# A two-layer hybrid trunk on one core: conditioning loads on GpSimd's queue, output products behind the inner products of their turn, half a unit between the token transposes

## The chip, the cores and the metric

The kernel runs on one core of a Trainium2 chip. A core has five engines with one instruction stream each: TensorE (PE; its weight loads are listed as PEld), VectorE (DVE), ScalarE (ACT), GpSimd (POOL) and SyncE (SP). Each works through its own stream in order, and waits on semaphores where an instruction needs the result of another engine. Transfers are issued from an engine's stream and run on 16 DMA engines that are shared by all streams.

The metric is the device time of one execution in microseconds (us). A difference is judged from several runs of both kernels on the same chip.

## The reference

One sequence of 256 tokens of width 1024 goes through two layers. Each layer has three sub-layers: a feed-forward block (SwiGLU), a token mixer, and a second feed-forward block. The mixer of layer 0 is HGRN2, a gated linear recurrence with eight heads; that of layer 1 is a chunked gMLP. All sub-layers have the same frame, where shift, scale and gate come from a vector c of the sequence:

```
cond = silu(c)
mod = (cond @ ada_w[i] + ada_b[i]).reshape(B, 3 * N_SUB, D_MODEL)[:, :, None, :]
...
def swiglu(h, w_in, w_out):
    a, b = jnp.split(h @ w_in, 2, axis=-1)
    return (jax.nn.silu(a) * b) @ w_out

def sublayer(x, fn, pre_g, post_g, shift, scale, gate, res_w):
    h = rms_norm(x, pre_g) * (1.0 + scale) + shift
    return x + res_w * gate * rms_norm(fn(h), post_g)
```

The computation of `mod` is called the conditioning here. Its weights are 1024 x 9216 numbers for each layer, and each is used once. All data are float32.

## The kernel before

**Sub-layers.** The six sub-layers are called ffn0, hg, ffn1, ffn2, gm and ffn3, and are worked off one after the other. The 256 tokens are two tiles of 128 (t = 0, 1). Between two sub-layers stands the seam: `tail` scales the output y and adds it to x for each token tile, and `prenorm` normalizes x, transposes it on PE (`npa`), applies scale and shift on ACT (`hf`, L243) and splits it into two parts (`h`, L247 and L248).

**Products in split form.** Float32 operands are split into a rounded part (hi) and the rest (lo), and a product is hi*hi + hi*lo + lo*hi. A weight block of 1 MB comes as two loads of 512 KB into `raw` (4 buffers); ACT casts each into the hi part (L119), and DVE subtracts to get lo (L120). `next_block` (`nb`) hands out the blocks in the order in which the host laid them out. Split blocks lie in the pool `whl` of 12 tiles, two tiles a block.

**Conditioning.** It is 144 products: a tile of 128 outputs x 1024 weights (512 KB, `ada`) is loaded, and DVE multiplies it with `cond` and sums along the row (L169), which gives one column of `mod`. `pace(upto, blocks, skip)` sets a rate, and `wblock` calls `ada` at that rate, so that the products are written between the weight blocks. All loads of weights and of conditioning are issued by SP through `load` (L55), and `keep_in_program_order` holds each behind whatever was traced before it on the same engine. The conditioning tiles lie in the pool `adap` of two buffers; the first 16 products also use the four buffers of `p4` for two tiles out of three (`ring`). The HGRN2 gate's scratch tile `L` (L526) takes its buffers from `adap` too.

**A feed-forward layer.** The inner width of 2816 is cut into 11 units of 256. In ffn0 the units 0 to 3 are made in eight steps over the inner dimension, as the conditioning of the first norm arrives. In ffn1, ffn2 and ffn3 the units 0 and 1 are made by `proj` with the tokens as rows, since token tile 0 is ready before tile 1; it fills the four PSUM banks of the pool `acc`. `post_tok` then takes silu and product, token tile by token tile, and transposes the result on PE (`tps`, L396) into the form that the output product needs; ACT and DVE split it (L147, L148). The other units go through `unit2`, a generator with two steps: each makes two chunks of 128 columns (`chunk2`, the `ups` matmuls of L328 and L329), whose banks are read by ACT and DVE (L377 to L382). After the inner products of a turn, `out()` adds an older unit's output products (`y`, L142 to L144) into four y banks, until no more than two units are pending:

```
for u in range(len(pend), 11):
    ...
    while len(pend) > 2:
        out()
```

In turn u == 8 `gate_tile` makes the gate of the sub-layer as a row: a transpose on PE (`gps`), a copy (`grow`), a transfer to memory (`gflat`, L199) and one that spreads the row over all partitions (`G`, L201). Both transfers are issued by POOL, which does nothing else after the start.

**What sets the order.** The semaphores and the order of each engine's instructions come from a planner that simulates the program: of the instructions whose operands are ready by its reckoning it takes the one written first, so an instruction may run far ahead of, or behind, its place in the program. `after` adds an edge of issue order alone. `paced` uses it: the first matmul of a group is placed behind the instruction in `self.gate`, if one is set, and the gate is cleared.

Of the kernel before, what the change touches and what calls it, by code (L numbers as in the profile page):

```python
# [10 lines left out]
F32 = mybir.dt.float32  # L11
# [7 lines left out]
P = 128  # L19
D = 1024  # L20
S = 256
KC = D // P
# [11 lines left out]
class Body:  # L34
    def __init__(self, ctx, tc, ins, out):
        self.ctx, self.tc, self.nc, self.out = ctx, tc, tc.nc, out
        self.d = dict(zip(_INS, ins))
        pool = lambda name, bufs, **k: ctx.enter_context(tc.tile_pool(name=name, bufs=bufs, **k))
        self.const = pool("const", 1)
        self.raw = pool("raw", 4)  # L40
        self.whl = pool("whl", 12)
        self.act = pool("act", 1)
        self.adap = pool("adap", 2)
        self.cols = pool("cols", 2)
        self.tiny = pool("tiny", 4)
        self.bcp = pool("bcp", 2)
        self.p4 = pool("p4", 4)
        self.p2 = pool("p2", 4)
        self.scr = pool("scr", 1)
        self.acc = pool("acc", 4, space=PSUM)  # L50
        self.yps = pool("yps", 1, space=PSUM)
        self.dram = pool("dram", 2, space=bass.MemoryType.DRAM)
# [106 lines left out]
    def ada(self, upto):  # L159
        nc = self.nc  # L160
        while self.ada_next < min(upto, 144):
            i = self.ada_next
            if self.ring and i % 3:
                t = self.p4.tile([P, D], F32, tag="t4", name="ada")
            else:
                t = self.adap.tile([P, D], F32, tag="ada", name="ada")
            self.load(t, self.d["ada"][i])
            junk = self.scr.tile([P, D], BF16, tag="junkv", name="junkv")
            nc.vector.tensor_tensor_reduce(junk, t, self.cond, 1.0, 0.0, ALU.mult, ALU.add,  # L169
                                           self.mod[i // 24][:, i % 24:i % 24 + 1])  # L170
            self.ada_next += 1
# [150 lines left out]
    def chunk2(self, w, c):  # L322

        ps = self.acc.tile([P, 2, S], F32, tag="acc", name="ups")
        mm = self.nc.tensor.matmul
        for kc in range(KC):
            u = [x[:, kc * 256 + c * P:kc * 256 + (c + 1) * P] for x in w]
            self.paced(mm(ps, u[0], self.h2[:, :, :, kc, :], start=kc == 0, stop=False))  # L328
            mm(ps[:, 1, :], u[1], self.h2[:, 0, :, kc, :], start=False, stop=kc == KC - 1)  # L329
        return ps  # L330

    def mm3f(self, o, u, h, start, stop):
        mm = self.nc.tensor.matmul
        self.paced(mm(o, u[0], h[0], start=start, stop=False))  # L334
        mm(o, u[0], h[1], start=False, stop=False)  # L335
        mm(o, u[1], h[0], start=False, stop=stop)  # L336

    def gtile(self):

# [1 line left out]
        return [g[:, i * 512:(i + 1) * 512].rearrange("p (k s) -> p k s", k=2) for i in range(2)]  # L341

    def out_unit(self, y, gT, wo, first):
        for t in range(NT):
            for h in range(2):
                for k in range(2):
                    self.out_mm(y[t][h], t, h, gT, k, wo, k, first and k == 0, False)

# [9 lines left out]
    def ffn(self, f, hT, G_fn, pre_next, nxt, bg):  # L358
        nc = self.nc
        state = {"out": 0}  # L360
        nb = self.next_block
# [25 lines left out]

        def post_tok(pa, pb):
            gTs = [self.gtile() for _ in range(2)]
            for t in range(NT):  # L390
                sa = self.t2()
                self.tact(sa, pa[t], AF.Silu)
                nc.vector.tensor_mul(sa, sa, pb[t])
                ps = self.acc.tile([P, 512], F32, tag="acc", name="tps")
                for k in range(4):
                    nc.tensor.transpose(ps[:, k * P:(k + 1) * P], sa[:, k * P:(k + 1) * P], self.ident)  # L396
                pv = ps.rearrange("p (u k s) -> p u k s", u=2, k=2)
                for u in range(2):
                    self.split_ps(*[g[:, :, t * P:(t + 1) * P] for g in gTs[u]], pv[:, u])
            return gTs  # L400

        def out():
            self.out_unit(y, pend.pop(0), nb(), state["out"] == 0)
# [20 lines left out]
            self.late_consts()  # L424
        else:
            wa, wb = [[nb(), nb()] for _ in range(2)]
            pend = post_tok(*self.proj(hT, [wa, wb], 512, split=True))
        y = self.y_banks()
        self.pace(bg, 25 if f == 0 else 26)
        for u in range(len(pend), 11):  # L430
            if f == 0:
                pa = self.unit(hT, nb())
                pb = self.unit(hT, nb())
            else:
                steps = unit2(nb(), nb())
                next(steps)
                next(steps)
            while len(pend) > 2:
                out()
            if f == 0:  # L440
                pend.append(post(pa, pb))
            else:
                for _ in steps:
                    pass
            if u == 8:
                G = G_fn()
# [38 lines left out]
    def hgrn(self, hT, G_fn, pre_next, nxt, bg):  # L485
# [37 lines left out]

        def gate_f(hb, pr, z):

            L = self.adap.tile([P, 512], F32, tag="ada", name="L")  # L526
            c = slice(512 * pr, 512 * pr + 512)
            k, nk, b = kn[hb][:, c], kn[hb][:, H4:][:, c], bq[hb][:, c]
            nc.scalar.activation(L, z, AF.Abs)
# [246 lines left out]
    def gmlp(self, hT, G_fn, pre_next, nxt, bg):  # L776
# [12 lines left out]
            self.tact(o, o, AF.Gelu_apprx_tanh)  # L789

        v, vt = [], []
        self.pace(bg, 30, 6)
        for j in range(6):
            if j == 0:
                bbs = [bcast(self.t2(N), "gbin", N * i) for i in range(2)]
# [300 lines left out]
```

## Time and profile before

| | |
|---|---|
| time, median of 3 runs | 1191.67 us (1189.63 to 1193.36) |
| the profiled execution | 1193.24 us, span 1191.5 us |
| granted TensorE clock, mean | 0.984 |
| moved by DMA | 282.32 MB, mean 237 GB/s |
| conditioning loads | 144 of 512 KB, issued by SP |
| weight loads | 376 of 512 KB, issued by SP |

The span is the time from the first to the last instruction; the profiled execution's own time is 1.7 us longer. The profile gives the busy time of each engine, the transfers, the chain of work that ended last, and for each idle stretch of an engine who ended it. In such a row "PE y L142 <- ACT t L147: 4.5, 3, 2.4" says that PE, at the instruction of line 142 that writes y, waited for ACT's instruction of line 147 that writes t: 4.5 us in total, three times, 2.4 us at most. A timeline row has the start and the length in us, the engine, the line, the operation, what it writes and reads, and in brackets the idle time before it with who ended it. SPq and PEq are the sequencers of SP and PE.

### The profile page before, as it was taken

The page shows a single profiled execution, that of the slowest core. Times are in us where ns is not written, and L with a number is a line of the kernel's source. Part 1 is how long each engine was busy: PE and PEld are TensorE (multiplying, and loading weights), DVE is VectorE, ACT ScalarE, POOL GpSimd, SP SyncE. Part 2 cuts the span into 40 slices and gives each one's busy share as a digit, 9 for nine tenths or more (in the row PEclk, how much of TensorE's full clock was granted, in tenths as well). Part 3 has the DMA queues.
Part 4 walks back from the last instruction along what each step waited for, and adds up shares of the span by engine and source line. Part 5 has one row for each costly group of instructions (what it writes and reads, how often), then busy time and mean ns, then how long its engine had stood idle before and what let it go on. Part 6 is the DMA issues. An engine that isn't in the chain of part 4 may idle for free.

```text
span 1191.5 us, 17180 instructions
## 1 busy us (share of the span) xinstructions
PE 1146.5 (96%) x6518; PEld 995.4 (84%) x6518; DVE 888.8 (75%) x1331; ACT 657.2 (55%) x1054; POOL 6.8 (1%) x16
## 2 busy tenths in 40 slices
PE   7999999997997999999999999999999999999997
PEld 6999998797895788888778888888888887888886
DVE  6997888868887887787677787657978786666652
ACT  6464446648766754456655545554754457555541
POOL 0000000000000000000000000000000000000000
PEclk9999999997999999999999999999999999999999
DMA  9899998782335777887578888537777765666640
GB/s 345 311 314 318 333 327 314 251 285 101 124 95 185 263 267 272 278 272 262 173 251 267 282 269 272 188 124 261 277 254 262 248 212 177 203 222 233 213 137 36
DMA packets 79765, 282.32 MB, mean 237 GB/s; under 512 B 9873, under 2 KB 10561, under 8 KB 79682
## 3 DMA queue, kind: packets, MB, share of 16 engines
q1 hardware_dynamic: 78626, 278.05, 68.0%
q0 software_dynamic: 1056, 3.17, 0.8%
q8 instruction: 51, 0.84, 0.3%
q14 instruction: 32, 0.26, 0.1%
HBM read 280.11 MB, written 1.07 MB: 236 GB/s over the span
## 4 chain that ended last, share of the span: by engine, by line
PE 73%; DMA 10%; DVE 8%; ACT 5%; issue 3%; SPq 0%; DVEq 0%; ACTq 0%
PE ups L328 15%; PE ups L329 8%; PE y L144 7%; PE y L142 7%; PE y L143 7%; PE ups L418 4%; DMA ada<-in_ada 4%; DMA raw<-in_wffn 4%; DVE w L120 3%; PE ups L334 3%; PE ups L336 3%; PE ups L335 3%; DMA raw<-in_whg 3%; ACT w L119 2%; PE ab L599 2%
## 5 line engine op out<-in xcount | busy, mean ns | idle before, releaser
L120 DVE TENSOR_TENSOR w<-raw,w 128x1024 fp32r<-128x1024 f32 x376 | 453.5, 1220 | 84.7 <-ACT w L119 77.5
L119 ACT CAST w<-raw 128x1024 fp32r<-128x1024 f32 x376 | 388.0, 1050 | 202.9 <-DMA raw<-in_wffn 79.4
L328 PE MATMUL ups<-h,w 128*128 128x512 f32 x864 | 303.1, 394 | 0.0
L169 DVE CUSTOM_DVE_ANT_0 junkv<-ada,cond 128x1024 bf16<-128x1024 f32 x144 | 175.8, 1221 | 92.0 <-DMA ada<-in_ada 91.5
L329 PE MATMUL ups<-h,w 128*128 128x256 f32 x864 | 242.5, 281 | 0.0
L328 PEld LDWEIGHTS ups<-h,w 128*128 128x128 f32 x864 | 162.3, 188 | 36.8
L142 PE MATMUL y<-w,t 128*128 128x512 f32 x448 | 179.4, 400 | 4.5 <-ACT t L147 4.5
L143 PE MATMUL y<-w,t 128*128 128x512 f32 x448 | 178.2, 398 | 0.0
L144 PE MATMUL y<-w,t 128*128 128x512 f32 x448 | 177.6, 397 | 0.2
L329 PEld LDWEIGHTS ups<-h,w 128*128 128x128 f32 x864 | 163.7, 190 | 0.9
L334 PE MATMUL ups<-h,w 128*128 128x256 f32 x416 | 118.3, 285 | 0.6 <-ACT w L119 0.6
L336 PE MATMUL ups<-h,w 128*128 128x256 f32 x416 | 117.8, 283 | 0.2 <-DVE w L120 0.2
L335 PE MATMUL ups<-h,w 128*128 128x256 f32 x416 | 117.6, 283 | 0.0
L142 PEld LDWEIGHTS y<-w,t 128*128 128x128 f32 x448 | 84.5, 189 | 24.1 <-ACT t L147 5.3
L144 PEld LDWEIGHTS y<-w,t 128*128 128x128 f32 x448 | 84.3, 189 | 21.0 <-DVE t L148 1.1
L143 PEld LDWEIGHTS y<-w,t 128*128 128x128 f32 x448 | 84.5, 189 | 17.9
L79 ACT ACTIVATE t<-t 128x256 f32<-128x256 f32 (+2 forms) x70 | 36.3, 523 | 97.7 <-DVE t L378 95.5
L334 PEld LDWEIGHTS ups<-h,w 128*128 128x128 f32 x416 | 79.7, 192 | 1.7 <-ACT w L119 0.8
L335 PEld LDWEIGHTS ups<-h,w 128*128 128x128 f32 x416 | 79.7, 192 | 0.8 <-issue 0.2
L336 PEld LDWEIGHTS ups<-h,w 128*128 128x128 f32 x416 | 79.7, 192 | 0.4 <-DVE w L120 0.4
L291 PE MATMUL pps<-w,h 128*128 128x512 f32 x160 | 64.4, 403 | 5.3 <-DVE h L247 5.3
L292 PE MATMUL pps<-w,h 128*128 128x512 f32 x160 | 63.8, 399 | 0.0
(199 smaller groups left out, 1435.4 us busy)
## 6 DMA issues: line engine op xcount, KB each, us to landing
raw<-in_wffn SPq DMA_DIRECT2D x264, 512.0 KB, 5.5
ada<-in_ada SPq DMA_DIRECT2D x144, 512.0 KB, 6.5
raw<-in_wgmu SPq DMA_DIRECT2D x48, 512.0 KB, 5.2
raw<-in_whg SPq DMA_DIRECT2D x40, 512.0 KB, 5.8
raw<-in_wgmv SPq DMA_DIRECT2D x24, 512.0 KB, 5.0
G<-gflat POOLq DMA_DIRECT2D x6, 512.0 KB, 5.9
t<-in_gbin SPq DMA_DIRECT2D x6, 256.0 KB, 5.2
x<-in_x SPq DMA_DIRECT2D x2, 512.0 KB, 4.0
```

Of the source, the lines that this page charges most:

```text
L119: nc.scalar.copy(hi[:, sl], raw)
L120: nc.vector.tensor_sub(lo[:, sl], raw, hi[:, sl])
L142: self.paced(mm(ps, l[0], r[0], start=start, stop=False))
L143: mm(ps, l[0], r[1], start=False, stop=False)
L144: mm(ps, l[1], r[0], start=False, stop=stop)
L169: nc.vector.tensor_tensor_reduce(junk, t, self.cond, 1.0, 0.0, ALU.mult, ALU.add, self.mod[i // 24][:, i % 24:i % 24 + 1])
L291: mm(res[g][t], h(0, kc), u(0, kc), start=kc == 0, stop=False)
L328: self.paced(mm(ps, u[0], self.h2[:, :, :, kc, :], start=kc == 0, stop=False))
L329: mm(ps[:, 1, :], u[1], self.h2[:, 0, :, kc, :], start=False, stop=kc == KC - 1)
L334: self.paced(mm(o, u[0], h[0], start=start, stop=False))
L335: mm(o, u[0], h[1], start=False, stop=False)
L336: mm(o, u[1], h[0], start=False, stop=stop)
```

## The change

It has five edits.

- The conditioning loads are issued by POOL instead of SP, held in order among what POOL issues. The pool `adap` has three buffers instead of two.
- `L` of the HGRN2 gate has its own buffer in a new pool `lp` for the second pair of heads, and the scratch tile `hf` for the first.
- `chunk2` and `mm3f` note their last matmul in `self.last`. `out_unit` sets it as the gate before each group of output products, so that they are issued behind the inner products written last.
- In ffn1, ffn2 and ffn3 `post_tok` is a generator. The first step of unit 2 is written between the first and the second token tile; the turn of u == 2 then has only the second step left.
- The rates: ffn0 spreads its products over 22 weight blocks (before 25), the other feed-forward layers over 23 (before 26), with the rate set ahead of unit 2's blocks, and the gMLP layer over 27 (before 30).

```diff
-        self.adap = pool("adap", 2)
+        self.adap = pool("adap", 3)
+        self.lp = pool("lp", 1)
...
-            self.load(t, self.d["ada"][i])
+            self.tc.keep_in_program_order(nc.gpsimd.dma_start(t, self.d["ada"][i]))
...
-            mm(ps[:, 1, :], u[1], self.h2[:, 0, :, kc, :], start=False, stop=kc == KC - 1)
+            self.last = mm(ps[:, 1, :], u[1], self.h2[:, 0, :, kc, :], start=False, stop=kc == KC - 1)
...
-        mm(o, u[1], h[0], start=False, stop=stop)
+        self.last = mm(o, u[1], h[0], start=False, stop=stop)
...
     def out_unit(self, y, gT, wo, first):
         for t in range(NT):
             for h in range(2):
+                self.gate = self.last
                 for k in range(2):
                     self.out_mm(y[t][h], t, h, gT, k, wo, k, first and k == 0, False)
...
         def post_tok(pa, pb):
             gTs = [self.gtile() for _ in range(2)]
+            pend.extend(gTs)
             for t in range(NT):
...
-            return gTs
+                yield
...
             wa, wb = [[nb(), nb()] for _ in range(2)]
-            pend = post_tok(*self.proj(hT, [wa, wb], 512, split=True))
+            pend = []
+            self.pace(bg, 23)
+            tokens = post_tok(*self.proj(hT, [wa, wb], 512, split=True))
+            next(tokens)
+            steps = unit2(nb(), nb())
+            next(steps)
+            next(tokens)
         y = self.y_banks()
-        self.pace(bg, 25 if f == 0 else 26)
+        if f == 0:
+            self.pace(bg, 22)
         for u in range(len(pend), 11):
...
-                steps = unit2(nb(), nb())
-                next(steps)
+                if u > 2:
+                    steps = unit2(nb(), nb())
+                    next(steps)
                 next(steps)
...
-            L = self.adap.tile([P, 512], F32, tag="ada", name="L")
+            L = self.lp.tile([P, 512], F32, tag="L", name="L") if pr else self.scr.tile([P, 512], F32, tag="hf", name="L")
...
-        self.pace(bg, 30, 6)
+        self.pace(bg, 27, 6)
```

## The prediction

> **What bounds the kernel now.** I read the page first, then the busy time in stretches, the waits of each engine, and only then the chain of waits around the places that the first three point to.
>
> ```profile
> span 1191.5 us, 17180 instructions
> PE 1146.5 (96%) x6518; PEld 995.4 (84%) x6518; DVE 888.8 (75%) x1331; ACT 657.2 (55%) x1054; POOL 6.8 (1%) x16
> ```
>
> TensorE (PE) is idle for 1191.5 - 1146.5 = 45.0 us; no matmul is added or taken away, so nothing here can be worth more than that. The stretches tell where the idle time lies. The columns are the stretch, its length, then busy time and count of PE, its weight loads, VectorE (DVE), ScalarE (ACT) and GpSimd (POOL), then clock, DMA share and GB/s.
>
> ```profile
> 190.00:300.00 110.00, 99.88 (x628) 91.22 (x626) 87.25 (x144) 71.77 (x129) 0.00 (x0) 0.94 0.65 217
> 300.00:390.00 90.00, 82.03 (x487) 70.69 (x486) 75.20 (x129) 62.05 (x127) 1.07 (x2) 0.96 0.41 135
> ...
> 420.00:555.00 135.00, 135.00 (x722) 115.82 (x721) 102.38 (x149) 67.53 (x108) 1.08 (x2) 1.00 0.79 271
> 555.00:620.00 65.00, 59.54 (x261) 47.58 (x260) 46.57 (x73) 38.90 (x71) 0.00 (x0) 0.95 0.65 220
> ```
>
> The body of a feed-forward layer (420 to 555) leaves PE no gap at all: faster weights or products are worth nothing there. The time is lost at seams, where one sub-layer hands over to the next (555 to 620), and in the HGRN2 layer. Who ended PE's waits (us in total, times, longest):
>
> ```profile
> PE pps L291 <- DVE h L247: 5.3, 5, 2.3
> PE y L142 <- ACT t L147: 4.5, 3, 2.4
> ...
> PE npa L239 <- DVE xn L233: 3.2, 2, 2.1
> PE fps L336 <- DVE w L120: 3.1, 2, 1.7
> PE ab L599 <- DVE t L593: 3.0, 1, 3.0
> ...
> PE npa L239 <- ACT xn L235: 1.7, 2, 1.2
> PE vps L854 <- DVE t L861: 1.6, 2, 1.2
> PE tps L396 <- DVE t L393: 0.9, 1, 0.9
> PE fps L334 <- ACT w L119: 0.7, 1, 0.7
> ```
>
> These rows are the prices of what follows.
>
> **Part 1: the first turn of ffn1, ffn2 and ffn3 (output products gated, a unit's step between the transposes).** The three waits of y for the cast L147 are the three starts of these layers. The order in time for ffn2, on PE and on ACT:
>
> ```profile
> 606.30 0.60 PE L396 MATMUL tps<-ident,t 128*128 128x128 f32 x4
> 609.32 0.50 PE L142 MATMUL y<-w,t 128*128 128x512 f32 x1 [2.43 <-ACT t L147]
> ...
> 612.39 0.78 PE L328 MATMUL ups<-h,w 128*128 128x512 f32 x1
> ```
> ```profile
> 607.96 1.04 ACT L119 CAST w<-raw 128x1024 fp32r<-128x1024 f32 x1 [2.11 <-DMA raw<-in_wffn]
> 608.91 0.36 ACT L147 CAST t<-tps 128x256 fp32r<-128x256 f32 x1
> ```
>
> After token tile 0's transposes PE's next instruction is an output product, which needs L147; L147 stands on ACT behind a weight cast that waits 2.11 us for its DMA. The inner products (ups), whose operands are ready, are queued behind it until 612.39. The change forbids that order and traces half a unit between the transposes. That half is 32 matmuls (two chunks, eight k, two each), at 135 / 722 = 187 ns about 6.0 us: more than the 2.43 us that they have to cover, and than the 0.9 us for token tile 1's multiplication L393. So both rows go: 4.5 + 0.9 = **-5.4 us**. It adds no instruction and no semaphore, only issue order. What it needs is a PSUM bank: of the four "acc" banks the projection holds all, and two come free when token tile 0's silu and multiplication have read them, before its transposes; I see no reason for a new stall. Bounds: 0 (no bank, or the unit's weights late) to -5.4. In later turns, and in ffn0 and the gMLP layer, the gate orders only what the program order already has; where PE has no idle time there is nothing to lose, and I take 0. If a unit's weights came late there, the output products queued behind its last inner product would no longer fill in; that cover is the full PE of the 420 row.
>
> **Part 2: the conditioning loads leave SP.** The 144 products of the conditioning (L169) and their loads remain; each load is issued by POOL instead of SP. Waits of SP's queue, and of DVE for these loads:
>
> ```profile
> SPq L56 <- DVE w L120: 588.0, 246, 19.1
> ...
> SPq L56 <- DVE mod L169: 77.2, 42, 6.2
> ```
> ```profile
> DVE junkv L169 <- DMA ada<-in_ada: 91.5, 51, 5.4
> ```
>
> For 77.2 us SP stood at a conditioning load whose buffer a product had not freed, with weight loads behind it. Here is what that does at the seams, from the chain of waits (start, length, what):
>
> ```profile
> 198.03 1.23 DVE junkv L169
> ...
> 199.72 6.83 DMA raw<-in_whg
> ```
> ```profile
> 257.38 0.94 DVE junkv L169
> ...
> 258.97 5.01 DMA raw<-in_whg
> ```
> ```profile
> 565.03 6.61 DMA ada<-in_ada
> ...
> 571.66 1.23 DVE junkv L169
> ```
> ```profile
> 868.77 6.58 DMA ada<-in_ada
> ```
>
> At 565 the load went out behind weight loads; DVE stands until 571.66 in the middle of a tail, and PE pays the 2.1 us of the longest npa wait. With loads on their own queue, a third buffer, and the pace ended about three weight blocks sooner (23 for 26), the load is long there: **-2.1** (bounds 0 to -2.1). At 199.72 and 258.97 a weight load leaves only after a product has freed a buffer. The first ends in PE's longest wait for h (2.3) and in the one for ACT's xn (1.2); the weight buffers might hold these loads as well, so I take half of 3.5: **-1.7** (0 to -3.5). The second feeds the waits of fps (3.1 + 0.7); in that stretch ACT also loses 3.9 us because L, the gate's scratch, shares the two conditioning buffers, and the change gives L buffers of its own:
>
> ```profile
> ACT L L529 <- DVE mod L169: 3.9, 1, 3.9
> ```
>
> With either cause gone the weights come sooner by more than the 3.8 us: **-3.8** (0 to -6.8, if the 3.0 of L599 just after goes too). The wait at 868 is the vps row: **-1.6** (0 to -1.6). Moving L to the scratch tile "hf" makes it wait for the last prenorm, done by then: nothing; without that it would be the same 3.9.
>
> The pace (22 for 25, 23 for 26, 27 for 30 blocks) moves products and changes no count. The issue costs POOL, idle 99%, about what its own loads of the same 512 KB cost:
>
> ```profile
> 156.12 0.65 POOL L199 DMA_DIRECT2D gflat<-grow  x1 [155.67 <-ACT grow L197]
> 162.88 0.56 POOL L201 DMA_DIRECT2D G<-gflat  x1 [6.11 <-DMA gflat<-grow]
> ```
> ```profile
> ada<-in_ada SPq DMA_DIRECT2D x144, 512.0 KB, 6.5
> G<-gflat POOLq DMA_DIRECT2D x6, 512.0 KB, 5.9
> ```
>
> 144 x 0.56 = 81 us on an idle engine, and a landing no later than SP's: 0. By the Trainium skill's "DMA: Bandwidth & Descriptors", section "Issuing engines are not separate DMA queues", loads of all issuers interleave on the same 16 DMA engines and a second issuer saves issue time only; the two landing times agree with that. If no more than this were gained, the sum would be part 1 alone; rival A gives that time from rows.
>
> At the start, up to seven conditioning tiles now compete with x and the first weights. The first read of x waits for something else:
>
> ```profile
> 6.32 1.22 DVE L905 CUSTOM_DVE_ANT_0 xn<-x 128x1024 f32<-128x1024 f32 x1 [5.33 <-PE cps L897]
> ```
>
> A load issued at 1.2 us has 5 us to land, the 5.9 of the POOL row is close to it: **+0.5** (0 to +2).
>
> **What comes in.** The loads were paced because SP's order held them between weight blocks. On POOL nothing holds them but buffers and the G loads. The planner fills idle engine time from far ahead, as the first dates of gate (DVE) and of its transpose (PE), both written in one function, show:
>
> ```profile
> L192 DVE TENSOR_TENSOR gate<-mod,adab x6: 159/162/167, 103.2 to 1110.1; 128x8 f32<-128x8 f32 x6
> ```
> ```profile
> L195 PE MATMUL gps<-ident,gate x6: 271/275/275, 155.2 to 1134.5; 128*8 128x128 f32 x6
> ```
>
> 52 us ahead. So products can float into the attention stretch 300 to 390, which had next to none, where DVE idles 90 - 75.2 = 14.8 us: room for 12 of 1.23 us. Each that stands before something PE waits for delays it by 0.6 us on average; with half of them so, 6 x 0.6 = **+3.7** (0 to +14.8, all twelve in full).
>
> **Sum:** -5.4 - 2.1 - 1.7 - 3.8 - 1.6 + 0.5 + 3.7 = -10.4 us. The profiled execution took 1193.24 us (span 1191.5 and 1.7 around it), 1.6 over the median of the three runs, 1191.67. So 1182.8 for such an execution and **1181 us** for the median.
>
> **Rivals** (all on the median).
> A. The queue buys nothing: SP waits 588.0 us for its own weight buffers against 77.2, so a weight load freed from a product waits for L120 instead, and seams stay. Against it: at 565 it is the conditioning load itself that is late. Part 1 alone: 1191.7 - 5.4 = 1186.
> B. The change does not do what it says in part 1: no bank or no weights for the unit's step between the transposes, PE waits as before. Against it: the ups at 612.39 start without a wait of their own. 1181 + 5.4 = 1187.
> C. All twelve products get in the way of attention: 1181.3 + 14.8 - 3.7 = 1192, no change. For it, the 52 us; against it, that idle time is spread in short pieces.
> D. Slower: conditioning loads traced after a G load stand behind it on POOL. G waits for its row's round trip: 0.65 + 6.11 + 0.56, then 6.5 to land, 13.8 us without a tile. A unit of three blocks takes 88 matmuls x 187 ns = 16.5 us, so with 28 products on 23 blocks there is one every 4.5 us, and three tiles cover 13.5: just enough. If floating products have drained the tiles, DVE stands with the weight splits behind it. The body hides such a stand:
>
> ```profile
> 504.57 6.80 DMA ada<-in_ada
> ```
>
> This one cost PE nothing (420 row). From 6.8 us on it decides: 13.8 - 6.8 = 7.0 us at each of the gates of ffn0, ffn1 and ffn2, 21 us; the gains that hang on early products are lost, part 1 and the 3.8 stay: 1191.7 - 9.2 + 21 = 1203.
>
> **How the numbers follow.** Forecast 0.50, A 0.17, B 0.08, C 0.11, D 0.14. A difference under 0.3% (3.6 us, so 1188.1 to 1195.2) can't be told from no change. Faster: 0.47 of the forecast, 0.13 of A, 0.06 of B, 0.02 of C: 0.68. Slower: D almost whole, 0.13, and 0.03 from the upper ends of A and C: 0.16. Same: 0.16. The forecast's own range is 1172 (all bounds at their best: -5.4 - 2.1 - 3.5 - 6.8 - 1.6 = -19.4) to 1188. The range for 8 in 10 takes in A, B, C and D with two gates instead of three (1197): 1171 to 1198.
>
> **What would show it.** Part 1: no row of y for L147, and half a unit's ups between the two groups of tps. Part 2: SP's row for L169 gone, the row of junkv for its load far below 91.5, no load in the chain at 565 and 868, fps rows gone. Rival C shows as products between 300 and 390 and longer waits of ab there; D as long waits of junkv just after each G issue, with PE rows in the bodies that now have none. If PE's idle time falls little though these waits go, or a fresh seam opens with another releaser, my reading of the seams is wrong.

## The result, and the profile after

The changed kernel takes 1256.77 us (1254.64 to 1259.32), beside 1191.17 us for the kernel before on the same chip: 1.055 times as long, 95% interval 1.0521 to 1.058. It is slower by about 65 us, where 10 us less was forecast; the time lies far outside the range, 1171 to 1198.

The head of the page after:

```profile
span 1256.6 us, 17264 instructions
PE 1162.8 (93%) x6518; PEld 1003.7 (80%) x6518; DVE 885.7 (70%) x1331; ACT 661.7 (53%) x1054; POOL 82.6 (7%) x160
```

The work is the same: 6518 matmuls on PE, 1331 instructions on DVE. PE's idle time rose from 45.0 to 1256.6 - 1162.8 = 93.8 us, which is 48.8 of the 65.1 us of span. The other 16.3 us are the same matmuls taking longer in total (1162.8 for 1146.5 us), which goes with a lower mean granted clock, 0.972 for 0.984 over the span and lower still in stretches around the new stalls, as shown further below.

Who ended PE's waits (us in total, times, longest):

```profile
PE xps L933 <- ACT xn L929: 8.9, 1, 8.9
PE pps L292 <- DVE h L248: 8.7, 8, 2.8
PE ots L675 <- DVE t L670: 8.7, 2, 4.4
PE y L143 <- ACT t L148: 8.2, 3, 5.4
PE vps L866 <- ACT w L864: 7.7, 1, 7.7
PE vps L866 <- DVE t L873: 7.2, 3, 2.9
PE ups L329 <- DVE t L149: 7.1, 3, 3.3
PE npa L240 <- DVE xn L234: 5.5, 1, 5.5
PE tps L400 <- DVE t L397: 5.1, 3, 1.7
```

No single wait explains 49 us. There are many, all longer than before or new, at the start (xps), in the last turns of ffn0, ffn1 and ffn2 (y), in the tails (npa), in attention (ots), in the gMLP layer (vps), and at the first turns (ups and tps, three times each). Of the rows in which the prediction looked for its gains, only three moved as it said: the fps rows fell from 3.8 to 0.4 us, and the two that follow. The npa, vps, y and tps rows all grew. SP's wait for a conditioning product is gone; its first row now is the weights' own:

```profile
SPq L57 <- DVE w L121: 794.2, 297, 26.5
```

DVE's waits for conditioning tiles halved, from 91.5 us in 51 places:

```profile
DVE junkv L170 <- DMA ada<-in_ada: 46.3, 24, 5.8
```

What did change is when the 144 products run. The busy tenths of the products alone, in 40 equal slices of the span, first of before and then of after:

```profile
busy tenths in 40 slices 2422322230000122220022221000111200000000
```
```profile
busy tenths in 40 slices 3224014320011320002330001100123100000000
```

Before, they are spread over the bodies of the feed-forward layers (the runs of 2), with a pause in the HGRN2 layer. After, they come in heaps with empty stretches between, and several heaps stand at seams. In windows of the products alone (the stretch, its length, DVE's busy time and count, clock, DMA share, GB/s), before:

```profile
300.00:390.00 90.00, 1.23 (x1) 0.96 0.41 135
570.00:670.00 100.00, 18.33 (x15) 0.97 0.69 235
900.00:1000.00 100.00, 12.22 (x10) 1.00 0.67 225
```

and after:

```profile
300.00:390.00 90.00, 7.29 (x6) 0.94 0.47 157
570.00:670.00 100.00, 31.72 (x26) 0.97 0.81 287
900.00:1000.00 100.00, 26.85 (x22) 0.93 0.79 275
```

These windows are the same times, not the same stages, since after runs some 40 us late by ffn1's tail. Set to the stage, the 60 us around the start of ffn1's tail (30 before it and 30 behind) hold 4 products before and 18 after; around ffn0's tail it is 14 and 18.

What a heap does in a tail is seen on DVE in ffn0's tail of after (start, length, engine, line, what; in brackets the idle time before, and who ended it):

```profile
223.16 1.23 DVE L170 CUSTOM_DVE_ANT_0 junkv<-ada,cond 128x1024 bf16<-128x1024 f32 x1 [2.13 <-DMA ada<-in_ada]
...
226.16 1.23 DVE L170 CUSTOM_DVE_ANT_0 junkv<-ada,cond 128x1024 bf16<-128x1024 f32 x1 [1.69 <-DMA ada<-in_ada]
...
227.31 0.16 DVE L225 RECIPROCAL r<-sq 128x1 f32<-128x1 f32 x1
...
227.97 1.40 DVE L266 SCALAR_TENSOR_TENSOR x<-yg,r,x 128x512 f32<-128x512 f32 x2
```

The reciprocal that the whole residual waits for stands behind two products on DVE, and these wait for their loads. ACT, and then PE, wait in turn (5.5 us, the npa row):

```profile
228.75 0.63 ACT L217 ACTIVATE junka<-x 128x512 bf16<-128x512 f32 x1 [7.15 <-DVE x L266]
```

The next table is for orientation. It gives the start of an instruction on PE, read from PE's rows: of before in us, and of other kernels how much later or earlier. The labels are those of the experiments.

| start on PE of | before | after | x1 queue alone | x2 rest alone | x4 products in place | x12 all held | x14 free again |
|---|---|---|---|---|---|---|---|
| first y | 75.6 | +13.7 | +13.1 | -0.2 | +7.4 | -0.1 | +1.1 |
| ffn0's tail (npa) | 204.7 | +28.2 | +24.6 | +1.6 | +10.6 | -0.8 | +28.0 |
| attention's output (ots) | 343.9 | +24.4 | +28.7 | -4.6 | +2.0 | -7.0 | +37.7 |
| ffn1's tail | 576.8 | +40.8 | +44.0 | -0.9 | +4.1 | -12.7 | +49.1 |
| ffn2's tail | 770.6 | +45.6 | +54.4 | -1.8 | +6.9 | -16.6 | +44.1 |
| 96th vps (gMLP) | 975.6 | +63.8 | +76.6 | +0.5 | +13.5 | -14.2 | +44.3 |
| end | 1191.5 | +65.2 | +76.9 | +4.3 | +17.9 | -16.1 | +42.8 |

### The profile page after: what moved, and what is told of

Its sections match the earlier page's. It is cut to its first block, busy times and chain, and to the rows that moved or that the text cites. A ratio compares the mean times of both kernels' runs of the same rounds, so it can differ in the third digit from the quotient of the medians.

```text
span 1256.6 us, 17264 instructions
## 1 busy us (share of the span) xinstructions
PE 1162.8 (93%) x6518; PEld 1003.7 (80%) x6518; DVE 885.7 (70%) x1331; ACT 661.7 (53%) x1054; POOL 82.6 (7%) x160
## 3 DMA queue, kind: packets, MB, share of 16 engines
q1 hardware_dynamic: 57890, 202.54, 47.3%
q0 software_dynamic: 21792, 78.68, 17.9%
## 4 chain that ended last, share of the span: by engine, by line
PE 64%; DMA 13%; issue 11%; DVE 7%; ACT 3%; POOL 1%; SPq 0%; DVEq 0%; POOLq 0%; ACTq 0%
PE ups L329 14%; DMA ada<-in_ada 8%; PE ups L330 7%; PE y L143 6%; PE y L145 6%; PE y L144 6%; PE ups L422 4%; DMA raw<-in_wffn 4%; DVE w L121 3%; PE ups L335 2%; PE ups L336 2%; PE ups L337 2%; PE ab L611 2%; PE pps L144 1%; PE pps L143 1%
## 5 line engine op out<-in xcount | busy, mean ns | idle before, releaser
L329 PE MATMUL ups<-h,w 128*128 128x512 f32 x864 | 306.6, 399 | 7.1 <-DVE t L149 7.1
L329 PEld LDWEIGHTS ups<-h,w 128*128 128x128 f32 x864 | 163.5, 189 | 46.7 <-issue 8.0
L143 PE MATMUL y<-w,t 128*128 128x512 f32 x448 | 181.2, 405 | 8.2 <-ACT t L148 8.2
L145 PE MATMUL y<-w,t 128*128 128x512 f32 x448 | 180.2, 403 | 0.4 <-DVE t L149 0.3
L144 PE MATMUL y<-w,t 128*128 128x512 f32 x448 | 179.7, 401 | 0.0
L330 PEld LDWEIGHTS ups<-h,w 128*128 128x128 f32 x864 | 164.2, 190 | 0.8
L143 PEld LDWEIGHTS y<-w,t 128*128 128x128 f32 x448 | 85.8, 192 | 28.9 <-ACT t L148 9.5
L168 POOL DMA_DIRECT2D ada<-in_ada x144 | 76.1, 530 | 449.1 <-DVE mod L170 306.9
L145 PEld LDWEIGHTS y<-w,t 128*128 128x128 f32 x448 | 85.8, 192 | 22.3 <-DVE t L149 2.0
L144 PEld LDWEIGHTS y<-w,t 128*128 128x128 f32 x448 | 86.0, 192 | 18.5
L335 PEld LDWEIGHTS ups<-h,w 128*128 128x128 f32 x416 | 81.7, 196 | 7.0 <-ACT t L80 5.2
L336 PEld LDWEIGHTS ups<-h,w 128*128 128x128 f32 x416 | 81.5, 196 | 0.8 <-issue 0.2
L337 PEld LDWEIGHTS ups<-h,w 128*128 128x128 f32 x416 | 81.5, 196 | 0.4 <-DVE w L121 0.4
L293 PE MATMUL pps<-w,h 128*128 128x512 f32 x160 | 63.8, 399 | 0.0
```

Source lines behind the costliest of these rows:

```text
L143: self.paced(mm(ps, l[0], r[0], start=start, stop=False))
L144: mm(ps, l[0], r[1], start=False, stop=False)
L145: mm(ps, l[1], r[0], start=False, stop=stop)
L168: self.tc.keep_in_program_order(nc.gpsimd.dma_start(t, self.d["ada"][i]))
L330: self.last = mm(ps[:, 1, :], u[1], self.h2[:, 0, :, kc, :], start=False, stop=kc == KC - 1)
L337: self.last = mm(o, u[1], h[0], start=False, stop=stop)
```

## The experiments

**Which half costs the time.** x1 is the kernel before with only the loads on POOL's queue; x2 is the change with the loads put back on SP.

```diff
 x1 (against before)
-            self.load(t, self.d["ada"][i])
+            self.tc.keep_in_program_order(nc.gpsimd.dma_start(t, self.d["ada"][i]))
 x2 (against after): the same line the other way round
```

> Before with one edit: the conditioning loads are issued by POOL, two buffers as before. Theory Q (the queue move is the whole loss: on POOL nothing paces the loads, they run as far ahead as the buffers and the last G load let them, and their products pile up at the start and at the seams): 1240 to 1255. Theory S (the sum of the other edits is to blame, the queue is neutral or a gain as predicted, -9.2 by its terms): 1180 to 1192.

> After with one edit undone: the conditioning loads go back to SP; gate, half unit, third buffer, L's own buffers and the paces stay. Theory Q: 1180 to 1200, the 65 us gone. Theory S: 1240 or more. The profile after shows each start of ffn1 to ffn3 with about 4 us of PE waits where before had 2 to 3, so even by Q I expect no gain from the first turn: 1190 to 1200.

x1 took 1269.53 us, 1.0652 (1.0601 to 1.0702). x2 took 1194.55, 1.0013 (0.9992 to 1.0034). So the one line with the queue costs some 77 us by itself, more than Theory Q's range, and the rest of the change gives no difference.

**The products in their written order.** x4 is the change with one more hold: DVE issues each product behind the instruction that was written before it.

```diff
-            nc.vector.tensor_tensor_reduce(junk, t, self.cond, ...)
+            self.tc.keep_in_program_order(nc.vector.tensor_tensor_reduce(junk, t, self.cond, ...))
```

> After with one edit added: each product L169 is held on DVE behind the instruction that was written before it, so that it cannot run ahead of its place. Loads stay on POOL. Theory F (floating: what hurts is products that run ahead on DVE, and the loads that they pull): 1190 to 1205. Theory H (the queue itself hurts: loads beside the weight loads on the 16 DMA engines, issue by POOL, the wait behind G): still 1235 or more.

1215.05 us, 1.0186 (1.0145 to 1.0228), 10 us above Theory F's range and far below Theory H's. Of the 5.5% two thirds are gone, 42 us. The loads are still on POOL; the one edit fixes where the products stand on DVE, and with it when their buffers come free for the next loads.

**The start.** In x4 the first output product was still 7.4 us late. In the changed kernel DVE's first instructions are these:

```profile
7.54 1.23 DVE L170 CUSTOM_DVE_ANT_0 junkv<-ada,cond 128x1024 bf16<-128x1024 f32 x1 [0.26 <-DMA ada<-in_ada]
...
11.14 0.17 DVE L940 TENSOR_SCALAR ab<-adab 128x8 f32<-128x8 f32 x1 [1.22 <-DMA adab<-in_adab]
11.26 1.23 DVE L170 CUSTOM_DVE_ANT_0 junkv<-ada,cond 128x1024 bf16<-128x1024 f32 x1
...
13.99 1.22 DVE L170 CUSTOM_DVE_ANT_0 junkv<-ada,cond 128x1024 bf16<-128x1024 f32 x1
...
15.14 0.48 DVE L927 TENSOR_SCALAR xn<-x,r 128x512 f32<-128x512 f32 x1
```

Before, the same scaling of x by r was this row:

```profile
9.37 0.49 DVE L915 TENSOR_SCALAR xn<-x,r 128x512 f32<-128x512 f32 x1
```

After, four products stand ahead of it, and the bias `adab` is late. x5 is x4 with the first 16 loads back on SP.

```diff
-            self.tc.keep_in_program_order(nc.gpsimd.dma_start(t, self.d["ada"][i]))
+            if i < 16:
+                self.load(t, self.d["ada"][i])
+            else:
+                self.tc.keep_in_program_order(nc.gpsimd.dma_start(t, self.d["ada"][i]))
```

> The change with the products kept in the written order, and the first 16 conditioning loads left on SP's queue; the rest of them stays on POOL's. Theory (the start's loss comes from the first loads, which on POOL's own queue share the DMA engines with the token row, the biases and the first weights): the start's +7.4 us of the run with the products in place is gone, first inner product at 16.0 to 17.0 us and first output product at 75 to 77 us, time 1206 to 1209. Rival (the products' fixed order makes the start late): the first output product stays near 83 us, time 1213 to 1217.

1214.63 us, 1.0165 (1.0107 to 1.0224). The start is mended (first output product at 75.5 us, 0.2 earlier than before), but ffn0's tail comes 10.7 us late all the same, and the time is that of x4. Half a miss: the cause of the late start was right, its worth was not. What is lost ahead of ffn0's tail is lost there whether the start is late or not. The trace of x5 shows it as one wait of PE of 9.13 us for ACT's L148, at 201.51 us; where it comes from is taken up with x12.

**The gate rows.** What was left stood around the tails and the gMLP layer. There the transfers of the gate row (`gflat`, `G`) share POOL's queue with the loads. x6 is x4 with both transfers issued by SP. x7 is the kernel before with the loads on POOL from the seventeenth on, the products in the written order, and the gate rows on SP.

```diff
-        nc.gpsimd.dma_start(flat, row)
+        nc.sync.dma_start(flat, row)
...
-        nc.gpsimd.dma_start(G, flat.rearrange(...)...)
+        nc.sync.dma_start(G, flat.rearrange(...)...)
```

> x4 (after with the products held in place) with the two transfers of the gate row issued by SP instead of POOL, so that no conditioning load stands behind them. In x4 the stretch from the first output product to the first transpose of the ffn0 tail is 3.2 us longer than before, and that from the hg-like start of gm's products to the end of the gMLP turns 6.7 us longer, each just after a G load when three conditioning loads go out at once. Theory G (the pile-up behind the gate row costs this): about 10 us less than x4, 1203 to 1208. If the loads' free run on the shared DMA engines costs it wherever they are: 1212 to 1218, as x4.

> Before, with the conditioning loads on POOL except the first 16, which stay on SP; products held in their written place on DVE; gate row transfers on SP. No other edit. If the loss of x1 is made of floating products, the start and the gate row alone, this stands at before: 1188 to 1197. If issue by POOL costs something by itself (two queues sharing the DMA engines, weight loads late): 1200 or more.

x6 took 1277.98 us, 1.0713 (1.0661 to 1.0765), and x7 1278.88, 1.0704 (1.0655 to 1.0752). Both are plain misses, and the reason is in SP's waits, here of x6:

```profile
SPq L201 <- ACT grow L199: 164.4, 5, 38.1
```

On SP the row stands at the head of the weights' queue and waits there for ACT to make it, up to 38 us, with all later weights behind it. The edit moved the barrier to a worse queue. So the next two take it off both: x10 is x7 with the rows on POOL again, and x11 is x7 with the rows issued by ACT, which makes them.

```diff
 x10
-        nc.sync.dma_start(flat, row)
+        nc.gpsimd.dma_start(flat, row)
 x11
-        nc.sync.dma_start(flat, row)
+        nc.scalar.dma_start(flat, row)
 (and the G transfer likewise)
```

> The kernel before with the conditioning loads on POOL's queue from the seventeenth on and the products in the written order; gate rows stay on POOL. Nothing else of the change. Theory (what is left of the queue's cost once order and start are held is the gate row, which stands in POOL's queue and lets the loads behind it out together): weights late after each G, 3 us in the tail of ffn0 and 6 to 7 us at the gm stage, time 1199 to 1203. Rival 1 (the queue held in this way costs nothing and saves SP's waits): 1185 to 1192. Rival 2 (the loads as such ahead of the weights, wherever the rows are): 1203 to 1212.

> As the run with the queue held and the rows on POOL, but both gate-row transfers are issued by ACT, which makes the row; so neither SP's weights nor POOL's loads stand behind it. Theory (gate row as a barrier; on SP it held the weights 164 to 185 us): no wait on the row in any queue but some 2 us of ACT for each of the six rows, time 1188 to 1194, 6 to 12 us below the run with the rows on POOL. Rival (the barrier costs nothing on POOL): equal to that run within 3 us.

x10 took 1224.34 us, 1.0241 (1.0189 to 1.0292), slower than any of the three forecasts had it, and x11 1202.98, 1.0076 (1.0048 to 1.0103). Taking the row off POOL is worth 21 us, more than the 6 to 12 expected; x11 itself is 9 us above its range. POOL's rows of x10 show the barrier:

```profile
130.90 0.53 POOL L170 DMA_DIRECT2D ada<-in_ada  x1 [5.10 <-DVE mod L172]
160.10 0.52 POOL L203 DMA_DIRECT2D gflat<-grow  x1 [28.67 <-ACT grow L201]
162.93 0.53 POOL L205 DMA_DIRECT2D G<-gflat  x1 [2.31 <-DMA gflat<-grow]
163.45 1.05 POOL L170 DMA_DIRECT2D ada<-in_ada  x2
```

and the same stretch of x11 has a load every three to six us:

```profile
131.16 0.53 POOL L170 DMA_DIRECT2D ada<-in_ada  x1 [3.92 <-DVE mod L172]
135.73 0.53 POOL L170 DMA_DIRECT2D ada<-in_ada  x1 [4.04 <-DVE mod L172]
...
156.94 0.53 POOL L170 DMA_DIRECT2D ada<-in_ada  x1 [2.89 <-DVE mod L172]
```

For 29 us of ffn0's body, where a product costs nothing, x10 issues no load. The loads go out afterwards, on the way to ffn0's tail, which comes 18.5 us late in x10 and 7.8 us late in x11. In x10 DVE also stands 9.2, 6.5 and 5.6 us for the first conditioning load behind the gate rows of ffn0, ffn1 and ffn2, at the first of them in this row:

```profile
174.08 1.23 DVE L172 CUSTOM_DVE_ANT_0 junkv<-ada,cond 128x1024 bf16<-128x1024 f32 x1 [9.16 <-DMA ada<-in_ada]
```

**One cause or two.** x13 is the change as it was made, products free, with only the gate rows moved to ACT.

> The change as it was made, products free, with one edit: the two transfers of each gate row are issued by ACT instead of POOL. Theory A (one cause: the row in POOL's queue holds the loads back and lets them out together, and the products only pile up for that reason): bursts after G are gone, time 1200 to 1220. Theory B (two causes that add: free products 42 us, row 21 us): 1230 to 1240. Theory C (the row does not matter while products float): 1250 to 1260.

1261.18 us, 1.0554 (1.0522 to 1.0587): the third theory, a microsecond above its range. While the products may float, the row does not matter. The last of the 144 starts at 556 us in x13 and at 990 us in the change; the row in POOL's queue merely stops them at each gate on their way ahead.

**Everything held, and one hold released.** x12 is the whole change with the products in their written order, the first 16 loads on SP, the gate rows on ACT, and the reordered silu described further below. x14 is x12 with the products free again.

```diff
 x14 (against x12)
-            self.tc.keep_in_program_order(nc.vector.tensor_tensor_reduce(junk, t, self.cond, ...))
+            nc.vector.tensor_tensor_reduce(junk, t, self.cond, ...)
```

> The whole change, with the silu of the second token tile written ahead of the half unit, the products in the written order, the first 16 loads on SP and the gate rows on ACT. Theory (with order, start, row and silu mended the two ideas add up): the run with the rows on ACT less the 13 us that the silu and the gate were worth together, 1175 to 1182. Rival (the paced SP queue is worth more than its waits cost): above the same kernel with the loads on SP (1178.5), 1185 to 1200.

> The version with everything held (silu first, products in order, first 16 loads on SP, rows on ACT; 1177 us), with the products free again. Theory A (products pile up only behind the gate row on POOL): within 5 us of it, 1175 to 1183. Theory B (free products cost by themselves): 1205 to 1225.

x12 took 1177.22 us, 0.9854 (0.9821 to 0.9887), 1.5% faster than before. It also settles x5: up to ffn0's tail the two kernels differ only in the engine that issues the gate row. In x5 the tail is 10.7 us late, and POOL stands at that row:

```profile
159.81 0.52 POOL L204 DMA_DIRECT2D gflat<-grow  x1 [27.37 <-ACT grow L202]
```

In x12, with the row on ACT, the tail is 0.8 us early.

x14 took 1234.08, 1.033 (1.0299 to 1.036), above Theory B's range: 57 us for one hold on one instruction. The products of x14, in slices, are all done by 580 us of 1234:

```profile
busy tenths in 40 slices 2413444244001223323000000000000000000000
```

The worst place shows how it costs. At the end of ffn0, DVE of x14:

```profile
200.11 1.23 DVE L173 CUSTOM_DVE_ANT_0 junkv<-ada,cond 128x1024 bf16<-128x1024 f32 x1 [1.66 <-DMA ada<-in_ada]
...
207.70 0.08 DVE L173 DVE_READ_ACCUMULATOR2_ANT mod<- 128x1 f32 x1
207.70 0.68 DVE L373 TENSOR_TENSOR t<-t,ups 128x512 f32<-128x512 f32 x1
```

and PE, which waits for the cast of what L373 makes:

```profile
193.21 0.40 PE L145 MATMUL y<-w,t 128*128 128x512 f32 x1
209.09 0.80 PE L143 MATMUL y<-w,t 128*128 128x512 f32 x1 [15.48 <-ACT t L148]
209.68 0.63 PE L144 MATMUL y<-w,t 128*128 128x512 f32 x1
```

ACT had finished the silu that L373 multiplies by at 198.62 us; the multiplication ran nine us later. Six products in the fourteen us up to 208 stand before or between weight splits and the multiplication, at a time when their loads and the weights' share the DMA engines. In 200 to 220 the products' window reads (clock, DMA share and GB/s last):

```profile
200.00:220.00 20.00, 9.79 (x8) 0.58 0.98 363
```

**Does the queue buy anything.** x15 is x12 with all loads back on SP.

```diff
-            if i < 16:
-                self.load(t, self.d["ada"][i])
-            else:
-                self.tc.keep_in_program_order(nc.gpsimd.dma_start(t, self.d["ada"][i]))
+            self.load(t, self.d["ada"][i])
```

> The version with everything held (1177 us), with all 144 conditioning loads back on SP's queue; products stay in the written order, gate rows on ACT, silu first. Theory (the queue buys nothing once the products keep their place, since SP's place in the order and a product's place in the order are the same pace): 1174 to 1180. Rival (the queue does buy the 9.9 us that were forecast for it): 1184 to 1190. Third: the queue costs by itself, 1165 to 1172.

1176.28 us, 0.9875 (0.9847 to 0.9904), level with x12. With the products held, the queue buys nothing that these runs can tell. SP of x15 still has its stands at conditioning loads, and they cost nothing that can be measured:

```profile
SPq L57 <- DVE mod L170: 58.5, 46, 7.6
```

**The first turn.** x3 is the kernel before with the gate and the half unit alone. x3b is the kernel before with the gate alone.

```diff
 x3b
-            mm(ps[:, 1, :], u[1], ...)
+            self.last = mm(ps[:, 1, :], u[1], ...)
...
+                self.gate = self.last
 x3 (beside these): post_tok as a generator, and
+            next(tokens)
+            steps = unit2(nb(), nb())
+            next(steps)
+            next(tokens)
```

> Before with the gate of the output products and the half unit between the transposes, nothing else. Prediction's term: -5.4, so 1186. Rival theory B (banks: the half unit's second chunk waits for the bank that the transposes hold until they are split, and the second transposes wait for their multiplication): three starts at 3.9 to 5.4 us of waits in place of 1.7 to 3.2, so +2 to +7, 1193 to 1198.

> The kernel before with only the gate of the first turn: output products wait for the inner products of their turn; no half unit, loads on SP. By the prediction's split of its 5.4 us, the waits of the output products on ACT's silu at the first turns (0.8, 2.4 and 1.3 us) go: 1186 to 1189. Rival (the gate moves the wait to the first inner products or the transposes, as the half unit did): 1190 to 1196.

x3 took 1199.96 us, 1.0052 (1.003 to 1.0073), and x3b 1199.09, 1.0053 (1.0034 to 1.0071). Neither gains; both lose some 6 us, which puts x3 two us and x3b three above their rivals' ranges. In x3b PE stands at the second group of transposes, since the output products that ran meanwhile are now held back:

```profile
PE tps L397 <- DVE t L394: 11.6, 3, 4.6
```

In x3 the half unit is there, and two other waits are, here for ffn2, on PE:

```profile
612.65 0.77 PE L328 MATMUL ups<-h,w 128*128 128x512 f32 x1 [2.62 <-DVE t L148]
...
619.80 0.66 PE L398 MATMUL tps<-ident,t 128*128 128x128 f32 x4 [1.68 <-DVE t L395]
```

The half unit's second chunk waits for L148, the last reader of token tile 0's transposes, and the second transposes wait for token tile 1's multiplication L395, whose silu runs very late on ACT:

```profile
618.15 0.37 ACT L382 COPY t<-ups 128x256 f32<-128x256 f32 x1 [3.73 <-PE ups L329]
618.42 0.60 ACT L79 ACTIVATE t<-pps 128x512 f32<-128x512 f32 x1
```

ACT stood 3.73 us for the half unit's second chunk, with the silu, ready long before, behind that copy. So x8 is x3 with both tiles' silu and multiplication written ahead of the first transposes; x9 is x2 with the same edit; x16 is the kernel before with that edit alone.

```diff
+            sas = []
             for t in range(NT):
                 ...
                 nc.vector.tensor_mul(sa, sa, pb[t])
+                sas.append(sa)
+            for t in range(NT):
+                sa = sas[t]
                 ps = self.acc.tile([P, 512], F32, tag="acc", name="tps")
```

> x3 (first turn alone) with the silu and the multiplication of token tile 1 written ahead of the half unit, so that only the transposes and their splits come after it. Theory O (order on ACT: in x3 this silu stands behind the half unit's copies, so the bank of its input stays taken, the half unit's second chunk waits 2.6 to 3.9 us for the transposes' bank, and the second transposes wait 1.7 us): both waits go, and the prediction's -5.4 appears: 1185 to 1190. Theory B (four banks are too few for the half unit in any order): waits stay, 1195 to 1201.

> x2 (after with the loads on SP) with the same rewrite as x8. x2's marks stand 6.4 us ahead of before at the end of the hg layer and lose 5.6 at the next start; with the starts mended by Theory O: 1178 to 1187, faster than both kernels. By Theory B as x2: 1192 to 1197.

> The kernel before with only the silu and the multiplication of both token tiles written ahead of the first transposes; no gate, no half unit, loads on SP. Theory (the half unit needs the silu out of its way, and the gain is the two together): the output products still wait for ACT's cast at the three starts, 1189 to 1196, no change. Rival (the order of the silu is the whole gain): 1182 to 1186.

x8 took 1184.54 us, 0.9932 (0.99 to 0.9964); x9 1178.49, 0.9873 (0.9835 to 0.991); x16 1194.52, 1.0013 (0.9993 to 1.0032). The order of the silu alone is worth nothing, the gate and the half unit without it cost 6 us, and all together save 8. In x8 the silu of token tile 1 runs on ACT at

```profile
597.67 0.59 ACT L79 ACTIVATE t<-pps 128x512 f32<-128x512 f32 x1
```

and of PE's two waits at these starts one is gone and one is small (in x3 it was 9.1 us in three places):

```profile
PE ups L328 <- DVE t L148: 1.7, 3, 1.1
```

The faster versions x9, x12 and x15 can't be told from each other. x9 has its products free, with the loads on SP, and loses nothing by it.

## Why the prediction was wrong, point by point

**The term for floating products, +3.7, is the step that failed.** The prediction saw the mechanism: on POOL "nothing holds them but buffers and the G loads", and the planner runs far ahead. It then bounded the price by the DVE time that attention has left, 14.8 us, as if attention were the only place where a product may stand, and took half of half of it. Measured, the freedom costs 42 us in the change (after against x4) and 57 us in the mended version (x14 against x12). By the table, after is 17.6 us behind x4 at ffn0's tail, 22.4 at `ots` and 47.3 at the end; x14 is 28.8, 44.7 and 58.9 us behind x12. So the layer in which the prediction placed the whole price took 4.8 and 15.9 us of it up to attention's output. The rest is lost in ffn0, the tails, the seams and the gMLP layer, where one product is not a delay of its 1.22 us alone: it waits for its load at DVE's head, and weight splits, the reciprocal and the multiplication wait behind it. Nor was the loads' even spread an accident that could be given away. SP's order kept it: a conditioning load could not leave before the weight loads written ahead of it. Free products with the loads on SP cost nothing (x9 against x15, 0.9873 and 0.9875); with the loads on POOL they cost 57 us.

**Rival C** had this mechanism and a price of 14.8 us, for the same narrow place. **Rival D** named the barrier on POOL, which exists. Where the products are held, its 21 us come out (x10 against x11), and so does its sign: DVE stands 9.2, 6.5 and 5.6 us behind the gates of ffn0, ffn1 and ffn2, for which it had 7.0 each. What it had too small is the hold: it counted 13.8 us for the row's round trip, and POOL of x10 stands 28.67 us at the first row before that, waiting for ACT to make it. That the sum came out all the same is in part luck, since loads that go out late, into the tail, cost as well, and the two were not told apart. In the change itself the barrier adds nothing (x13); that products which float are already out of place is the likely reason.

**The gains of part 2, -2.1, -1.7, -3.8 and -1.6, are not the queue's.** Held in order, the queue is worth nothing (x12 against x15). That was rival A's reading, with a chance of 0.17: SP's waits for its own buffers take the place of those for the products (its wait for the split, 588.0 us before, is 734.7 in x12). The sentence of the Trainium skill that the prediction weighed ("DMA: Bandwidth & Descriptors", section "Issuing engines are not separate DMA queues") agrees with that pair of runs; it says nothing of the order that a queue keeps, on which the result hung. Only the fps term clearly came in, and without the queue: in x2, which has L in a buffer of its own and the loads on SP, `ots` comes 4.6 us earlier than before though fps began 4.4 us later. x2 also has the third buffer and the new pace; which of the three did it was not tried. The term of -1.6 was read too large as well: of the two vps waits only the longer, 1.2 us, follows the load at 868.

**The start, +0.5 with an upper bound of 2,** measured 13.7 us at the first output product. The prediction asked when x lands, and x was read no later (6.05 us for 6.32); it did not ask what DVE does before it scales x: four products of 1.22 us stand ahead, and the scaling is 5.8 us late. Of the late `adab`, the queue is the cause as well, since the loss goes when the first 16 loads are on SP (x5). This error did not decide: x14 has its start mended in this way (+1.1) and is as late at ffn0's tail as the change, 28.0 us for 28.2.

**Part 1, -5.4.** "What it needs is a PSUM bank" is the step that failed: the transposes take one of the two free banks, and the half unit has two chunks. That the second chunk's bank is the one the transposes held is inferred from its releaser, L148. x8 shows that both waits go when token tile 1's silu and multiplication come first; as this frees that tile's two banks and also takes its silu out from behind the half unit's copies, it does not tell the two reasons apart. With the silu moved, the two edits save 8 us, more than the 5.4. So the gain needs an edit that the change didn't have. Rival B, which had no bank for the unit's step, was the right reading of this part; x3's extra 6 us, a loss in place of no gain, it did not foresee. That the output products of the three first turns would no longer wait for the cast held: x2 and x3 show no such row, and the 8.2 us in after stand in the last turns of ffn0, ffn1 and ffn2. But the time came back as ups and tps rows (7.1 and 5.1 us in after).

**The bound of 45.0 us,** PE's idle time, took the busy time as fixed. It is not: the same 6518 matmuls take 1146.5 us before, 1162.8 after and 1136.8 in x12, whose gain is 6.5 us of idle time and 9.7 us of shorter matmuls.

**What was right.** Issuing 144 loads on POOL costs an idle engine about what was said: busy 82.6 - 6.8 = 75.8 us for 81. The row for L169 on SP went, and the fps rows fell to 0.4 us. None of this could make up for the rest.

**What stays open.** In x11 the held queue still costs 9 us, and in x12 nothing. Of this 7.8 us are lost by ffn0's tail, ahead of the layer that uses L, so L's buffer is not the reason there; the pace (fewer blocks), the third buffer and the gate of the output products are left and were not tried one by one. Nor is it settled how the 42 and 57 us divide: the hold on the products also fixes when their loads go out, so a product that stands in DVE's way and loads that share the DMA engines with the weights' at a bad time go together in all these runs.

## What to carry to other kernels

A load that stands in another stream's queue is paced by it, as the 144 loads were by SP's weight loads. Before it is given a queue of its own, ask what else fixes the place of the load and of its consumer, and pin the consumer; the time spent waiting at the head of the old queue is not by itself a loss. On an in-order queue, anything that waits for a late result is a barrier for all behind it: such a transfer belongs on the engine that makes the result. And when work is written between two steps to fill a gap, count the buffers that it takes, and look what it is put ahead of on the other engines.

## What the runs showed of the hardware that was not expected

A stall costs more than its length, since the matmuls after it are slower. In x14 the granted clock was 0.58 in the 20 us in which PE restarted after 15.48 us of idle time, and PE's rows there take 0.63 us where they took 0.40 just before it. Over the span the changed kernel spent 16.3 us more in the same 6518 matmuls, a quarter of its loss, which no row of waits shows; the prediction priced waits alone. The Trainium skill has the mechanism ("TensorE: Matmul & The Clock Gate", section "Part 1: The HAM clock gate"): an idle window puts the array at half rate, and sustained work lifts it again. The drop agrees. How long it lasts can be read from PE's rows in the tail of ffn0: after 5.38 us of idle time in the changed kernel the output products start 0.43 us apart from 211.62 to 217.40 us, and 0.23 us apart from there on; in x14 the slow rows last from 209.09 to 216.97.

One weight load took longer to land than the 5.0 to 6.8 us of the rows before. In x4's gMLP stage three conditioning loads leave POOL just behind the gate row, and a weight load issued some four us after them stands in the chain of waits for 10.58 us. That the burst is the reason is not shown: SP issues eight weight loads in the same stretch, and the median landing of these weights is 5.2 us in x4 as before.

```profile
851.90 1.57 POOL L168 DMA_DIRECT2D ada<-in_ada  x3
```
```profile
857.66 10.58 DMA raw<-in_wgmu
```
